# One more seven-product unit in the up-projection of an encoder trunk

## The chip, the cores and the metric

The kernel runs on one core of one Trainium2 chip. The metric is the device time of one launch in microseconds (us); lower is better. An execution under the hardware profiler gives the trace that all readings come from.

## The reference, cut to what matters

A trunk of two layers over 256 positions of width 2048, all in float32. Layer 0 mixes tokens with grouped-query attention, layer 1 with dilated window attention; each is followed by a gated MLP. Only the MLP's first step is touched by the change:

```python
def conv_ffn(h, w_up, conv_w, conv_b, w_down):
    u = h @ w_up                       # [256, 2048] @ [2048, 2 * 5632]
    u = depthwise_conv3(u, conv_w) + conv_b
    gate, val = split(u, 2)
    return (silu(gate) * val) @ w_down

for i in range(2):                     # layers
    h = h + mixer_i(rms_norm(h))
    h = h + conv_ffn(rms_norm(h), ...)
```

## The kernel before

**Three matmuls for one product.** Every float32 operand is split into two parts, a high one (`wh`, `xh`) and the rest (`wl`, `xl`). A product is then three matmuls on TensorE (PE), written in lines 135 to 137: `xh*wh`, `xh*wl`, `xl*wh`. The activations are the operand that is loaded into the array, the weights stream through it, 512 columns at a time. A weight tile of 128x1024 is loaded from memory by a DMA that SP issues into a tile `raw`; ScalarE (ACT) rounds it to `wh` (line 147), VectorE (DVE) subtracts to get `wl` (line 148). There are four `wh` and four `wl` tiles in rotation (`NHL`), so splits can run at most four tiles ahead of PE, and four `raw` tiles plus two extra ones.

**Tiling of the up-projection.** The 22 column blocks of 512 are taken as 11 pairs p, gate block p and value block 11+p. The first half has p = 0 to 5, the second 6 to 10; after each half the down-projection of that half runs. The inner dimension of 2048 is cut into four chunks kg of 512. In a plain pair (`project` twice, with `feed` for each chunk) the gate block runs through its four chunks and is handed to `gate_done`, then the value block does. One chunk of one block is 24 matmuls with 2 split weight tiles; of both blocks, 48 matmuls and 4 split tiles.

**The seven-product unit.** For the pairs in `UP` the function `up_pair` treats chunk 0 of gate and value together as a 2x2 block product in the Strassen-Winograd manner (`fast_unit`): seven products instead of eight. The activations' sums for it are made once per half, during p = 0 (lines 495 to 523, in the dictionary `picks`). The weights' four sums are made on DVE for every unit, in the `raw` tiles themselves (line 181), and each of the seven weight operands is split by ACT and DVE (lines 182 and 183). A unit is 42 matmuls (lines 189 to 191), 7 splits on each engine and 4 sums on DVE. Four of its products (numbers 1, 5, 6, 7) go to accumulators `ps` of their own; ACT copies number 1 out (line 547) and DVE folds them into the pair's four accumulators with eight additions (lines 549 to 557), so that the gate can be evacuated after the first four of these. The chunks run in `UP_ORDER`: gate chunks 1, 2, 3, the unit, value chunks 1, 2, 3.

**What else runs beside it.** `gate_gen` and `value_gen` are generators that are advanced a step at a time between the groups of matmuls: ACT evacuates an accumulator with the row's scale (line 492), DVE transposes 32x32 blocks (line 380), GpSimd (POOL) and ACT place them in `u` (line 632), ACT and DVE do the convolution (lines 612 and 620), ACT the silu (line 650), DVE the product with the gate (line 656) and the split of the result (ACT line 697, DVE line 698, or line 708 on where the chunk is one for a unit of the down-projection).

**What sets the order.** Each engine runs its own queue in order. The queue's order is made when the program is built, by a scheduler that follows the order in which the code emits; weight splits are emitted with a higher priority (`AHEAD`), so they stand earlier than the code says. `UP` also steers the generators: in `gate_gen` a gate in `UP` waits 3 steps (4 in one case) instead of 1 before the convolution of the value before it, and in `gate_done` such a gate goes into the list `beside`, which is advanced at other moments than `pending`.

Of the kernel before, what the change touches and what calls it, by code (L numbers as in the profile page):

```python
# [22 lines left out]
SCALE = 128.0 ** -0.5  # L23
NRAW, NHL = 4, 4
AHEAD = 60
UP = 2, 4, 6, 8
MIX = (0, 1), (0, 2), (1, 1), (1, 2)
MIX_ORDER = (1, 0), (2, 0), (3, 0), (1, 1), (2, 1), (0, None), (3, 1)
EVEN = range(0, 16, 2)
# [7 lines left out]
def tile_encoder(ctx: ExitStack, tc: tile.TileContext, x, xT, w_a, w_ao, q_gain, k_gain, w_b, w_bo,  # L37
# [265 lines left out]
    def project2(w, n0, n1, lhs, kgs, late, first_done, hook=None, cuts=(), drained=()):  # L303
        a0, a1 = new_acc(), new_acc()
        cuts = (0, *cuts, len(kgs) - late, len(kgs))
        for c0, c1 in zip(cuts, cuts[1:]):
            part, end = range(c0, c1), c1 == len(kgs)
            if end:
                drain()
                for gen in drained:  # L310
                    start(gen())
            for accs, n in ((a0, n0), (a1, n1)):
                for i in part:
                    kg = kgs[i]
                    mid = hook and hook(n == n0, kg)
                    feed(accs, lhs, kg, w[n, kg], i == 0, i == len(kgs) - 1,
                         pieces=4 if hook and i < 2 else 2 if hook else 1, mid=mid)
                if end and n == n0:
                    first_done(a0)
        return a1  # L320
# [204 lines left out]
    def up_pair(w, ns, lhs, order, picks, junk, fold_tile, first_done):  # L525
        (a2, a4), (a3, a8) = new_acc(), new_acc()
        acc, begun = {2: a2, 3: a3, 4: a4, 8: a8}, set()
        sides = (a2, a4), (a3, a8)
        tt = nc.vector.tensor_tensor
        for i, (kg, side) in enumerate(order):  # L530
            later = {s for _, s in order[i + 1:]}
            if side is None:
                acc.update({q: ps_tile() for q in (1, 5, 6, 7)})
                end = [q for q, s in ((1, None), (5, None), (6, None), (7, None), (2, 0), (4, 0), (3, 1))
                       if not later & {None, s}]
                fast_unit(acc, picks[kg], w[ns[0], kg], w[ns[1], kg], begun, end, None)
            else:
                mine = ((2, 4), (3, 8))[side]
                feed(sides[side], lhs, kg, w[ns[side], kg], not begun.issuperset(mine),
                     not later & {side, None}, begun=[m for m in range(2) if mine[m] in begun])  # L540
                begun.update(mine)
            if 0 in begun or not begun >= {1, 2} or later & {0, None}:
                continue
            begun.add(0)
            a, t = junk(), fold_tile()
            v, w_ = t[:, 0], t[:, 1]
            nc.scalar.activation(a, acc[1], AF.Copy)
            with tc.issue_after(newest[0].ins):
                tt(v, acc[6], a, ALU.subtract)
                tt(w_, acc[7], v, ALU.add)  # L550
                tt(a2, a2, a, ALU.add)
                tt(a4, a4, w_, ALU.subtract)
            first_done((a2, a4))
            tt(v, acc[5], v, ALU.add)
            tt(w_, acc[5], w_, ALU.add)
        tt(a3, a3, v, ALU.add)
        tt(a8, a8, w_, ALU.add)
        return a3, a8

    def ffn(l, hT, ss_in, cw, g_next, last, side=None):  # L560
        with tc.tile_pool(name=nm("fpool"), bufs=1) as fp:
# [63 lines left out]
            def turned(s, u, at_once=False):  # L625
                quad = quad_tile(fp, "quad", 2)
                for m in range(2):
                    quad_T(quad, slice(m, 8, 2), s[:, m])

                def move(i, put):  # L630
                    q, c = QC[i]
                    put(u[32 * c:32 * c + 32, :, :, 32 * q:32 * q + 32],  # L632
                        quad[32 * q:32 * q + 32, c].rearrange("p (j m) t -> p j m t", m=2))

                for i in range(0, 16, 2):
                    move(i, nc.gpsimd.tensor_copy)
                if not at_once:
                    yield
                for i in range(1, 16, 2):
                    move(i, partial(nc.scalar.activation, func=AF.Copy))  # L640

            def gate_gen(accs, blk, value):
                s = evac_scaled(fp, accs, rstd, 1)
                yield
                yield from turned(s, blk[1])
                if value is not None:
                    for _ in range(1 if blk[0] not in UP else 4 if value[5] // 4 - 1 in fast else 3):
                        yield
                    with tc.issue_after(evac[0].ins):
                        nc.scalar.activation(value[3], value[3], AF.Silu)  # L650
                    yield from product(value)
# [6 lines left out]
            def value_gen(accs, blk, gate, last):  # L658
# [10 lines left out]
                yield from turned(s, blk[1])  # L669
                wait = 5 if last is None or gate[0] + 1 in UP else 4 if gate[0] in UP else 2  # L670
                if gate[0] + 1 in UP and last is not None and last[5] // 4 in fast:
                    for _ in range(wait):
# [70 lines left out]
            for hf, (p0, p1) in enumerate(HALVES):  # L743
# [5 lines left out]
                for p in range(p0, p1):  # L749
# [5 lines left out]
                    def gate_done(accs, gate=gate, last_value=last_value):  # L755
                        gen = gate_gen(accs, gate, last_value)
                        if gate[0] in UP:
                            next(gen)
# [7 lines left out]
                    if p == 0:  # L766
                        va = project2(w_up[l], 0, NPAIR, hT, kgs, 1, gate_done, None, (), [first])
                    elif p in UP:
                        va = up_pair(w_up[l], (p, NPAIR + p), hT, UP_ORDER, picks, junk, st_tile, gate_done)
# [823 lines left out]
```

## Time and profile before

| | |
|---|---|
| median of 3 runs | 2221.86 us |
| the runs | 2221.15, 2221.86, 2224.96 us |
| span of the profiled execution, first to last instruction | 2220.5 us |
| PE busy | 2207.1 us (99%), 9933 matmuls |
| DVE busy | 1823.1 us (82%), 2295 instructions |
| ACT busy | 1528.2 us (69%), 2328 instructions |
| POOL busy | 546.1 us (25%) |
| DMA | 439.60 MB, mean 198 GB/s |

The profiled execution's own time is known only by its span; it is 0.65 us below the fastest of the three runs, which leaves room for no more than that around it. A row of groups reads: line, engine, operation, output<-inputs, shapes, count | busy time, mean ns of one | idle time just before them and what ended it. A timeline row gives the start in us from the span's start, the length in us, and the instruction, with xN for N of a kind in a row; idle time before it and its releaser stand in square brackets. Lengths of instructions on one engine overlap a little at their ends, so the distance of starts is shorter than the length; on PE it is much shorter. In the trace of layer 0, pair p = 1 begins at about 300 us and p = 2 at about 344 us; in layer 1 at about 1551 and 1594 us.

### The profile page before, as it was taken

What the parts mean: (1) busy time and instruction counts of PE and PEld (TensorE: products, weight loads), DVE (VectorE), ACT (ScalarE), POOL (GpSimd) and SP (SyncE); (2) the same over time, 40 slices, a digit from 0 to 9 for tenths busy, and PEclk for the clock granted to TensorE, in tenths of its full rate; (3) what the DMA queues carried; (4) which work ended last, traced back from release to release, by engine and by line L of the source; (5) the groups of instructions that cost most, each with busy time, mean ns of one, the idle gap of its engine ahead of it and who ended that gap; (6) DMA issues with size and microseconds to landing.
All of it is one profiled execution on the core that took longest, in us unless ns stands there. A gap on an engine that the chain in (4) does not pass through costs nothing.

```text
span 2220.5 us, 28992 instructions
## 1 busy us (share of the span) xinstructions
PE 2207.1 (99%) x9933; PEld 1828.5 (82%) x9933; DVE 1823.1 (82%) x2295; ACT 1528.2 (69%) x2328; POOL 546.1 (25%) x793
## 2 busy tenths in 40 slices
PE   9999999999999999999999999999999999999998
PEld 7888888888888888888888888888888888888887
DVE  6877669899897998868876878587798998879887
ACT  7666677787457787677756775567777855678764
POOL 3343222321003221042354216003222300212211
PEclk9999999999999999999999999999999999999999
DMA  8665665656656566665666555556555565656754
GB/s 305 192 220 184 216 188 190 201 189 196 203 181 222 186 205 200 204 202 195 183 199 199 174 180 189 190 184 214 181 202 194 192 209 190 217 162 218 224 193 143
DMA packets 126181, 439.60 MB, mean 198 GB/s; under 512 B 14408, under 2 KB 18248, under 8 KB 126032
## 3 DMA queue, kind: packets, MB, share of 16 engines
q1 hardware_dynamic: 123056, 429.05, 59.2%
q0 software_dynamic: 2688, 8.39, 1.5%
q8 instruction: 78, 1.28, 0.2%
q14 instruction: 71, 0.58, 0.1%
q10 hardware_dynamic: 288, 0.30, 0.0%
HBM read 432.34 MB, written 5.34 MB: 197 GB/s over the span
## 4 chain that ended last, share of the span: by engine, by line
PE 54%; POOL 1%; issue 1%; DMA 0%; ACT 0%; DVE 0%; POOLq 0%; DVEq 0%; ACTq 0%
PE acc L136 15%; PE acc L135 15%; PE acc L137 15%; PE ps L190 1%; PE ps L189 1%; PE ps L191 1%; PE acc L190 1%; PE acc L189 1%; PE acc L191 1%; DMA raw<-in_w_b_dram 0%; POOL wide L399 0%; PE ps L1422 0%; PE ps L342 0%; POOL wide L384 0%; ACT wh L147 0%
## 5 line engine op out<-in xcount | busy, mean ns | idle before, releaser
L148 DVE TENSOR_TENSOR wl<-raw,wh 128x1024 fp32r<-128x1024 f32 (+1 forms) x700 | 858.9, 1237 | 257.6 <-ACT wh L147 253.1
L147 ACT ACTIVATE wh<-raw 128x1024 fp32r<-128x1024 f32 (+1 forms) x700 | 726.8, 1046 | 342.5 <-PE acc L137 240.6
L136 PE MATMUL acc<-wl,xh 128*128 128x512 f32 x1984 | 773.8, 390 | 1.5 <-DVE wl L148 1.4
L135 PE MATMUL acc<-wh,xh 128*128 128x512 f32 x1984 | 773.7, 390 | 0.5 <-ACT wh L147 0.5
L137 PE MATMUL acc<-wh,xh 128*128 128x512 f32 x1984 | 772.1, 389 | 0.0
L136 PEld LDWEIGHTS acc<-wl,xh 128*128 128x128 f32 x1984 | 372.6, 188 | 81.5 <-DVE wl L148 5.7
L135 PEld LDWEIGHTS acc<-wh,xh 128*128 128x128 f32 x1984 | 372.5, 188 | 77.4 <-ACT wh L147 1.0
L137 PEld LDWEIGHTS acc<-wh,xh 128*128 128x128 f32 x1984 | 372.4, 188 | 76.9
L632 POOL COPY u<-quad 32x256 f32<-32x256 f32 x352 | 237.7, 675 | 702.5 <-DVE quad L380 684.4
L135 PE MATMUL acc<-wh,a 128*128 128x512 f32 x720 | 280.9, 390 | 0.0
L136 PE MATMUL acc<-wl,a 128*128 128x512 f32 x720 | 280.3, 389 | 0.0
L137 PE MATMUL acc<-wh,a 128*128 128x512 f32 x720 | 280.0, 389 | 0.0
L182 ACT ACTIVATE wh<-raw 128x1024 fp32r<-128x1024 f32 x140 | 148.5, 1061 | 122.4 <-PE acc L137 102.6
L183 DVE TENSOR_TENSOR wl<-raw,wh 128x1024 fp32r<-128x1024 f32 x140 | 166.9, 1218 | 6.3 <-ACT wh L182 5.8
L632 ACT ACTIVATE u<-quad 32x256 f32<-32x256 f32 x352 | 147.8, 420 | 23.2 <-DVE quad L380 18.7
L137 PEld LDWEIGHTS acc<-wh,a 128*128 128x128 f32 x720 | 135.1, 188 | 28.3 <-DVE a L331 0.2
L135 PEld LDWEIGHTS acc<-wh,a 128*128 128x128 f32 x720 | 135.2, 188 | 27.7
L136 PEld LDWEIGHTS acc<-wl,a 128*128 128x128 f32 x720 | 135.2, 188 | 27.6 <-DVE wl L148 0.3
L399 POOL COPY wide<-quad 32x256 f32<-32x256 f32 x88 | 54.8, 622 | 234.8 <-DVE quad L380 167.8
L492 ACT ACTIVATE stg<-acc,rstd 128x512 f32<-128x512 f32 x122 | 81.9, 685 | 32.9 <-PE acc L137 21.3
L384 POOL COPY wide<-quad 32x256 f32<-32x256 f32 x133 | 89.8, 675 | 41.4 <-DVE quad L380 32.0
L380 DVE STREAM_TRANSPOSE quad<-stg 128x512 f32<-128x512 f32 x112 | 75.7, 696 | 11.6 <-ACT stg L492 11.4
(318 smaller groups left out, 2444.5 us busy)
## 6 DMA issues: line engine op xcount, KB each, us to landing
raw<-in_w_up_dram SPq DMA_DIRECT2D x352, 512.0 KB, 4.6
raw<-in_w_down_dram SPq DMA_DIRECT2D x176, 512.0 KB, 4.6
raw<-in_w_b_dram SPq DMA_DIRECT2D x144, 512.0 KB, 4.6
raw<-in_w_bo_dram SPq DMA_DIRECT2D x48, 512.0 KB, 4.4
raw<-in_w_a_dram SPq DMA_DIRECT2D x40, 512.0 KB, 4.7
raw<-in_w_ao_dram SPq DMA_DIRECT2D x32, 512.0 KB, 4.5
raw<-in_w_a_dram SPq DMA_DIRECT2D x16, 256.0 KB, 5.8
there<-quad POOLq DMA_DIRECT2D x6, 512.0 KB, 3.7
```

Source lines behind the costliest of these rows:

```text
L135: nc.tensor.matmul(accs[m], xh, wh[:, j, :], start=st, stop=False)
L136: nc.tensor.matmul(accs[m], xh, wl[:, j, :], start=False, stop=False)
L137: nc.tensor.matmul(accs[m], xl, wh[:, j, :], start=False, stop=sp)
L147: nc.scalar.activation(wh[:, c], r[:, c], AF.Copy)
L148: newest[0] = nc.vector.tensor_tensor(wl[:, c], r[:, c], wh[:, c].bitcast(F32), ALU.subtract)
L182: nc.scalar.activation(wh, r, AF.Copy)
L183: newest[0] = nc.vector.tensor_tensor(wl, r, wh.bitcast(F32), ALU.subtract)
L380: nc.vector.transpose(quad[:, :, at, :], src.rearrange("p (x c t) -> p c x t", c=4, t=32))
L384: nc.gpsimd.tensor_copy(o[32 * c:32 * c + 32, :, 32 * q:32 * q + 32], quad[32 * q:32 * q + 32, c])
L399: nc.gpsimd.tensor_copy(dst, src)
L492: evac[0] = nc.scalar.activation(o[:, m, :], accs[m], AF.Copy, scale=rstd[:, m:m + 1])
L632: put(u[32 * c:32 * c + 32, :, :, 32 * q:32 * q + 32], quad[32 * q:32 * q + 32, c].rearrange("p (j m) t -> p j m t", m=2))
```

## The change

The tuple of pairs that go through `up_pair` gets a fifth member, 1:

```diff
-UP = 2, 4, 6, 8
+UP = 1, 2, 4, 6, 8
```

With it p = 1 of each layer goes through `up_pair` instead of two calls of `project`: one more unit per layer, two in the program. Pairs 1 and 2 are now both unit pairs, where before a plain pair lay between any two of them in the first half. In all, PE's queue has 12 rows fewer (9790 to 9778), DVE's 30 instructions more, ACT's 8 more. POOL's queue is the same; SP issues as many loads, eight of them from line 170 instead of line 125.

On DVE, in layer 0, this is what stands before where p = 1 reaches its last gate chunk (`cg`, `u`: the convolution of p = 0's gate):

```order
L148 TENSOR_TENSOR wl_3109<-raw_3092,wh_3108 128x1024
L148 TENSOR_TENSOR wl_3129<-raw_3124,wh_3128 128x1024
L620 SCALAR_TENSOR_TENSOR cg_2641<-u_2636,cw_555,cg_2641 128x256 x4
L148 TENSOR_TENSOR wl_3147<-raw_3126,wh_3146 128x1024
L620 SCALAR_TENSOR_TENSOR cg_2641<-u_2636,cw_555,cg_2641 128x256 x4
L148 TENSOR_TENSOR wl_3178<-raw_3173,wh_3177 128x1024
L148 TENSOR_TENSOR wl_3209<-raw_3175,wh_3208 128x1024
```

And at the same place in the changed program, where the unit of p = 1 now stands (`raw<-raw,raw` are the weights' sums):

```order
L148 TENSOR_TENSOR wl_3111<-raw_3092,wh_3110 128x1024
L183 TENSOR_TENSOR wl_3139<-raw_3130,wh_3138 128x1024
L181 TENSOR_TENSOR raw_3130<-raw_3130,raw_3136 128x1024
L181 TENSOR_TENSOR raw_3136<-raw_3136,raw_3134 128x1024
L183 TENSOR_TENSOR wl_3149<-raw_3132,wh_3148 128x1024
L183 TENSOR_TENSOR wl_3159<-raw_3134,wh_3158 128x1024
L181 TENSOR_TENSOR raw_3134<-raw_3130,raw_3134 128x1024
L181 TENSOR_TENSOR raw_3132<-raw_3134,raw_3132 128x1024
L183 TENSOR_TENSOR wl_3170<-raw_3130,wh_3169 128x1024
L183 TENSOR_TENSOR wl_3181<-raw_3136,wh_3180 128x1024
L183 TENSOR_TENSOR wl_3192<-raw_3134,wh_3191 128x1024
L183 TENSOR_TENSOR wl_3203<-raw_3132,wh_3202 128x1024
```

Eleven operations of 128x1024 take the place of four splits, and the gate's convolution has moved behind the unit.

On DVE, in the unit of p = 2 that follows, the order before was this (`wl_3515` is its first weight operand, `wl_3579` its last):

```order
L183 TENSOR_TENSOR wl_3515<-raw_3506,wh_3514 128x1024
L181 TENSOR_TENSOR raw_3506<-raw_3506,raw_3512 128x1024
L181 TENSOR_TENSOR raw_3512<-raw_3512,raw_3510 128x1024
L183 TENSOR_TENSOR wl_3525<-raw_3508,wh_3524 128x1024
L183 TENSOR_TENSOR wl_3535<-raw_3510,wh_3534 128x1024
L181 TENSOR_TENSOR raw_3510<-raw_3506,raw_3510 128x1024
L181 TENSOR_TENSOR raw_3508<-raw_3510,raw_3508 128x1024
L183 TENSOR_TENSOR wl_3546<-raw_3506,wh_3545 128x1024
L183 TENSOR_TENSOR wl_3557<-raw_3512,wh_3556 128x1024
L183 TENSOR_TENSOR wl_3568<-raw_3510,wh_3567 128x1024
L183 TENSOR_TENSOR wl_3579<-raw_3508,wh_3578 128x1024
```

In the changed program the same unit (now `wl_3540` to `wl_3604`) stands like this:

```order
L183 TENSOR_TENSOR wl_3540<-raw_3531,wh_3539 128x1024
L183 TENSOR_TENSOR wl_3550<-raw_3533,wh_3549 128x1024
L181 TENSOR_TENSOR raw_3531<-raw_3531,raw_3537 128x1024
L183 TENSOR_TENSOR wl_3560<-raw_3535,wh_3559 128x1024
L181 TENSOR_TENSOR raw_3537<-raw_3537,raw_3535 128x1024
L183 TENSOR_TENSOR wl_3571<-raw_3531,wh_3570 128x1024
L181 TENSOR_TENSOR raw_3535<-raw_3531,raw_3535 128x1024
L183 TENSOR_TENSOR wl_3582<-raw_3537,wh_3581 128x1024
L181 TENSOR_TENSOR raw_3533<-raw_3535,raw_3533 128x1024
L183 TENSOR_TENSOR wl_3593<-raw_3535,wh_3592 128x1024
L620 SCALAR_TENSOR_TENSOR cg_2993<-u_2635,cw_555,cg_2993 128x256
L183 TENSOR_TENSOR wl_3604<-raw_3533,wh_3603 128x1024
```

The eleven operations are the same, but each sum now stands directly ahead of the split that needs it, and a piece of a convolution has come in between.

On PE, at the end of that unit, the order before was (products number 6 in `ps`, then number 4 in `acc`, then the plain chunk of line 135):

```order
L189 MATMUL ps_3504<-wh_3567,s_2951 128x512
L190 MATMUL ps_3504<-wl_3568,s_2951 128x512
L191 MATMUL ps_3504<-wh_3567,s_2952 128x512
L189 MATMUL acc_3360<-wh_3578,xh_2293 128x512
L190 MATMUL acc_3360<-wl_3579,xh_2293 128x512
```

In the changed program two matmuls that need only a `wh` stand ahead of ones that need a `wl`:

```order
L189 MATMUL ps_3529<-wh_3592,s_2951 128x512
L189 MATMUL acc_3380<-wh_3603,xh_2293 128x512
L190 MATMUL ps_3529<-wl_3593,s_2951 128x512
L191 MATMUL ps_3529<-wh_3592,s_2952 128x512
L189 MATMUL ps_3529<-wh_3592,s_2951 128x512
L190 MATMUL ps_3529<-wl_3593,s_2951 128x512
L191 MATMUL ps_3529<-wh_3592,s_2952 128x512
L135 MATMUL acc_3381<-wh_3629,xh_2391 128x512
L190 MATMUL acc_3380<-wl_3604,xh_2293 128x512
```

The last product's first matmul with `wl_3604` has moved one place behind a matmul of the next chunk.

## Prediction

> **What bounds the kernel now.** I read the page's busy times first, then PE's row of the waits, then PE's timeline, and then DVE's windows, groups and timeline around p = 1 and p = 2.
>
> ```profile
> PE 2207.1 (99%) x9933; PEld 1828.5 (82%) x9933; DVE 1823.1 (82%) x2295; ACT 1528.2 (69%) x2328; POOL 546.1 (25%) x793
> ```
>
> PE is the bound: 99% of a span of 2220.5 us. The waits of PE over the whole program confirm it:
>
> ```profile
> PE ps L346 <- DVE qTl L331: 2.2, 2, 2.0
> PE ps L452 <- DVE warm L449: 1.5, 1, 1.5
> PE acc L136 <- DVE wl L148: 1.4, 4, 0.5
> PE acc L135 <- ACT wh L147: 0.5, 1, 0.5
> ```
>
> All visible waits of PE add to about 6 us. So a matmul that goes shortens the time, and a wait that comes lengthens it by its full size. The price of a matmul is not the 390 ns that its groups show, since matmuls overlap. It is the distance of starts:
>
> ```profile
> 329.68 0.39 PE L136 MATMUL acc<-wl,xh 128*128 128x512 f32 x1
> ...
> 342.37 0.39 PE L135 MATMUL acc<-wh,xh 128*128 128x512 f32 x1
> ```
>
> The second row is the 56th matmul after the first: 12.69 / 56 = 0.2267 us each.
>
> **What the change removes.** A chunk of a gate and value pair is 48 matmuls, a unit 42. Two units take away 12 matmuls, 12 x 0.2267 = 2.72 us, 0.12% of the time. That is the most that it can bring: 1.36 us in each layer. About 0.2% (4.4 us) is what a measurement of this kernel tells from no change, so a clear gain would need something beyond the removed matmuls, and I see nothing.
>
> **What it adds, on DVE.** The stretch that matters runs from where DVE would make the first split of the new unit (310.4 us in layer 0, 1560.7 in layer 1) to its last split for the unit of p = 2:
>
> ```profile
> core 0: us, DVE busy (x), PEclk, DMA share, GB/s
> 310.40:367.60 57.20, 45.51 (x57) 1.00 0.53 167
> 1560.70:1618.00 57.30, 45.47 (x57) 1.00 0.54 167
> ```
>
> DVE works 45.5 of 57.2 us there and idles 11.7. The groups of the same stretch tell the prices and the idle time:
>
> ```profile
> L148 DVE TENSOR_TENSOR wl<-raw,wh 128x1024 fp32r<-128x1024 f32 x16 | 19.8, 1243 | 10.7 <-ACT wh L147 10.7
> L183 DVE TENSOR_TENSOR wl<-raw,wh 128x1024 fp32r<-128x1024 f32 x7 | 8.2, 1218 | 0.0
> L181 DVE TENSOR_TENSOR raw<-raw,raw 128x1024 f32<-128x1024 f32 x4 | 4.9, 1225 | 0.1
> L698 DVE TENSOR_TENSOR a<-cv,a 128x256 fp32r<-128x256 f32 x4 | 1.7, 454 | 0.9 <-ACT a L697 0.9
> ```
>
> Step by step, for one layer:
> - Splits: seven for four, 3 x 8.2 / 7 = 3.5 us.
> - Sums of weights: 4 x 4.9 / 4 = 4.9 us.
> - Eight fold additions. In the unit of p = 2 they stand like this on DVE's timeline:
>
> ```profile
> 363.03 4.62 DVE L183 TENSOR_TENSOR wl<-raw,wh 128x1024 fp32r<-128x1024 f32 x4
> 367.57 0.69 DVE L551 TENSOR_TENSOR acc<-acc,junk 128x512 f32<-128x512 f32 x1
> ...
> 373.40 0.67 DVE L552 TENSOR_TENSOR acc<-acc,fold 128x512 f32<-128x512 f32 x1
> 373.97 0.67 DVE L554 TENSOR_TENSOR fold<-ps,fold 128x512 f32<-128x512 f32 x1
> 374.57 0.67 DVE L555 TENSOR_TENSOR fold<-ps,fold 128x512 f32<-128x512 f32 x1
> 376.81 0.71 DVE L380 STREAM_TRANSPOSE quad<-stg 128x512 f32<-128x512 f32 x1 [1.56 <-ACT stg L492]
> ```
>
>   Back to back they start 0.57 to 0.60 us apart, alone they take 0.69: 8 x 0.64 = 5.1 us.
>
> Together 13.5 us. The rest of DVE's work is the same set between the two places: convolution pieces stand later in the new order, but ahead of the same last split. So DVE needs 45.5 + 13.5 = 59.0 us, and has 57.2 - 1.36 = 55.8. It falls short by 3.2 us. It also had a lead to lose at the end:
>
> ```profile
> 368.50 0.39 PE L190 MATMUL acc<-wl,xh 128*128 128x512 f32 x1
> ```
>
> This is PE's first use of the unit's last `wl`; DVE had it at 363.03 + 4.62 = 367.65, so the lead was 0.85 us. PE's new order moves this use back by one matmul, 0.23 more. Unhidden remain 3.2 - 0.85 - 0.23 = 2.1 us per layer, if DVE does not idle for a moment. That is the lower end. DVE cannot save up for it: the splits run at most four tiles ahead, and the 10.7 us that it waited for ACT's `wh` were mostly waits for PE to free such a tile.
>
> The upper end adds the idle time that may survive. After the unit of p = 2, DVE waited 1.56 us for ACT to evacuate the gate (the row at 376.81), because ACT stood before a split whose weights had not landed:
>
> ```profile
> ACT wh L147 <- DMA raw<-in_w_up_dram: 3.8, 1, 3.8
> DVE quad L380 <- ACT stg L492: 1.6, 1, 1.6
> PEld acc L136 <- DVE wl L148: 0.9, 1, 0.9
> ```
>
> The unit holds four `raw` tiles to its end, so no load can start, and then they start late. On DVE and ACT the operations behind the new unit stand in the same order as behind that one, so I expect this wait of about 1.5 us again, now in a stretch that has no idle time to give. Another 0.9 is the wait for ACT's line 697. So DVE makes PE wait 2.1 to 2.1 + 1.5 + 0.9 = 4.5 us per layer. I take 3.7, the lower end with the first of the two waits: its place is the same, while convolution pieces now fill the second.
>
> **What hides.** The copies on ACT have these rows:
>
> ```profile
> L182 ACT ACTIVATE wh<-raw 128x1024 fp32r<-128x1024 f32 x140 | 148.5, 1061 | 122.4 <-PE acc L137 102.6 <-PE ps L191 8.4 <-issue 4.8
> L547 ACT ACTIVATE junk<-ps 128x512 f32<-128x512 f32 x12 | 7.0, 580 | 0.0
> ```
>
> A unit adds three copies and one evacuation, 3 x 1.06 + 0.58 = 3.8 us; ACT is busy 42.8 of the 57.2 us and has room:
>
> ```profile
> 310.40:367.60 57.20, 57.20 (x254) 47.22 (x253) 45.51 (x57) 42.82 (x63) 9.94 (x16) 1.00 0.53 167
> ```
>
> (The columns are the stretch, PE, weight loads, DVE, ACT, POOL.) If that cover were gone, its splits would be late by what is missing, and DVE's with them. SP issues as many loads, in another order; POOL's queue does not change. The sums of the activations are made for p = 2 already. The gate of p = 1 is ready 114 matmuls into the pair instead of 96; its accumulator is wanted by nobody before p = 2. The new unit itself should not make PE wait: it is entered with the lead that the unit of p = 2 had, and that one cost nothing.
>
> **The sum.** -2.72 + 2 x 3.7 = +4.7 us. The profiled execution spans 2220.5 us, 0.65 below the fastest run and 1.4 below the median of 2221.86; the sum against the span is 2225.2, and against the median that is compared, 2226.5 us. That is 0.2% slower, at the edge of what shows. With the two ends of the wait the time is 2221.86 - 2.72 + 2 x 2.1 = 2223.3, and 2221.86 - 2.72 + 2 x 4.5 = 2228.1.
>
> **The rivals.**
>
> *The cover holds.* DVE's 11.7 us of idle time are more than three quarters of the 13.5 us that are added, and part of the folds could slip behind the last split. If the lead carries the rest, the full 2.72 us stay: 2219.1. It decides whether DVE's added work ahead of the last split of p = 2 stays under 11.7 - 1.36 + 0.85 = 11.2 us. Against it: by the new order all of the 13.5 stand ahead.
>
> *Only the gap of the loads counts.* DVE keeps up, but each new unit costs the wait for the weights behind it. That was 0.9 us in layer 0 (the row of PEld above). Twice: -2.72 + 1.8, 2220.9. For it speaks that this wait is the only one of PE that the trace has near a unit here.
>
> *DVE slows while POOL copies.* Two spells of POOL's eight copies lie in the stretch of each layer. DVE and POOL at such places:
>
> ```profile
> 345.55 5.35 POOL L632 COPY u<-quad 32x256 f32<-32x256 f32 x8 [16.46 <-DVE quad L380]
> 377.65 7.40 POOL L632 COPY u<-quad 32x256 f32<-32x256 f32 x8 [26.75 <-DVE quad L380]
> ```
>
> ```profile
> 345.61 1.42 DVE L148 TENSOR_TENSOR wl<-raw,wh 128x1024 fp32r<-128x1024 f32 x1 [0.19 <-ACT wh L147]
> 368.17 2.35 DVE L148 TENSOR_TENSOR wl<-raw,wh 128x1024 fp32r<-128x1024 f32 x2
> ...
> 377.44 3.86 DVE L148 TENSOR_TENSOR wl<-raw,wh 128x1024 fp32r<-128x1024 f32 x3
> 381.23 2.22 DVE L620 SCALAR_TENSOR_TENSOR cg<-u,cw,cg 128x256 f32<-128x256 f32 x4
> ```
>
> ```profile
> 353.00 1.67 DVE L620 SCALAR_TENSOR_TENSOR cg<-u,cw,cg 128x256 f32<-128x256 f32 x4
> ```
>
> Where DVE had no gaps, behind 377, three splits took 3.86 us, against 1.5 x 2.35 = 3.53 without POOL, and four convolution pieces 2.22 against 1.67; POOL's copies stretched from 5.35 to 7.40. That is 0.9 us lost in one spell. With two such spells in a stretch that is now full, each layer loses up to 1.8 us more: 2226.5 + 3.6 = 2230.1. The page "SBUF — State Buffer" of the Trainium skill (section "SBUF: two separate sides") says that DVE operations with two inputs from SBUF and GpSimd operations share a port pair as an exclusive lock, and whichever starts second blocks for the whole instruction of the other. By that rule the sixteen copies of a stretch could hold DVE for all of POOL's 9.94 us, and the sum would be up to 2226.5 + 2 x 9.94 = 2246.4. The rows agree that there is a loss, though with 1.42 against 1.18 us for a split it is far less than a whole copy.
>
> **How the numbers follow.** The forecast (DVE short, 2223.3 to 2228.1 about 2226.5): 0.59. The cover holds, 2219.1: 0.12. Only the loads' gap, 2220.9: 0.11. POOL's slowing on top, 2230.1: 0.18. Slower by over 0.2% means over 2226.3: all of the last, and about half of the first, 0.47. Faster by over 0.2% is out of reach of 12 matmuls; 0.03 for runs that scatter. Within: 0.50. The range leaves out most of the case in which the cover holds, and ends just above the last: 2220.3 to 2231.0.
>
> **What would show it.** Right: PE with 9921 matmuls in rows 0.2267 us apart, a new wait of PE for DVE's `wl` of line 183 inside the unit of p = 2 (about 358 to 372 us, and 1250 us later in layer 1), 2 to 4 us in each layer, DVE busy without gaps from the new unit to there, and no new wait in the unit of p = 1. Wrong: PE without new waits (then DVE had more room than its rows say), a wait for DMA instead, or a wait in p = 3 or later, where I count none.

## The result, and the profile after

The changed kernel takes 2227.37 us (median of 21 runs, 2224.63 to 2229.3). The kernel before, run beside it, takes 2223.87 us (21 runs, 2221.15 to 2226.72; the three runs shown above are among these, two of them at its lower end). The ratio is 1.0014, 95% interval [1.0007, 1.0020]: slower by 3.1 us by the ratio and by 3.5 by the medians. I had predicted 2226.5 us. The interval leaves out 1, so 0.14% does show here; I had named 0.2% as the edge.

The profiled execution of the changed kernel spans 2225.1 us, and its time was 2226.85. In all its 21 runs the time is 1.7 to 1.8 us above the span. So the profile of before, with its span of 2220.5, was an execution of about 2222.3 us (an estimate from these), near the median of its three runs and not below the fastest. The busy times after:

```profile
PE 2207.5 (99%) x9921; PEld 1826.2 (82%) x9921; DVE 1850.2 (83%) x2325; ACT 1533.8 (69%) x2336; POOL 549.8 (25%) x793
```

PE has the 12 matmuls less. The span is longer all the same, and PE's waits over the whole program say for whom:

```profile
PE ps L346 <- DVE qTl L331: 2.5, 2, 2.0
PE ps L190 <- DVE wl L183: 2.4, 4, 0.6
PE acc L136 <- DVE wl L148: 1.8, 5, 0.6
...
PE acc L189 <- ACT wh L182: 1.3, 2, 0.7
```

Lines 189 and 190 are a unit; they were not in this list before. PE's timeline shows the place in layer 0, the unit of p = 2:

```profile
363.30 0.39 PE L189 MATMUL acc<-wh,s 128*128 128x512 f32 x1
363.96 0.50 PE L190 MATMUL acc<-wl,s 128*128 128x512 f32 x1 [0.27 <-DVE wl L183]
...
365.22 0.40 PE L189 MATMUL ps<-wh,s 128*128 128x512 f32 x1
366.23 0.50 PE L190 MATMUL ps<-wl,s 128*128 128x512 f32 x1 [0.61 <-DVE wl L183]
...
367.49 0.40 PE L189 MATMUL ps<-wh,s 128*128 128x512 f32 x1
368.50 0.50 PE L190 MATMUL ps<-wl,s 128*128 128x512 f32 x1 [0.61 <-DVE wl L183]
...
369.76 0.40 PE L189 MATMUL ps<-wh,s 128*128 128x512 f32 x1
370.81 0.50 PE L189 MATMUL acc<-wh,xh 128*128 128x512 f32 x1 [0.65 <-ACT wh L182]
```

The brackets understate the loss, since the matmul before counts as busy to its modelled end. The starts tell it: they stand 0.66, 1.01, 1.01 and 1.05 us apart where 0.227 is normal, and behind each of the four late matmuls the next start is about 0.335 us away, 0.11 more than normal. The excess is 3.25 us. In layer 1 the same sum is 2.80 us. So -2.72 + 3.25 + 2.80 = +3.3 us, and the runs say +3.1 to +3.5.

DVE, from the first split of the new unit to the last split of p = 2's unit (columns: the stretch, PE, weight loads, DVE, ACT, POOL, each with its count, then PEclk, DMA share, GB/s), has no room left:

```profile
312.29:372.25 59.96, 57.82 (x251) 46.61 (x250) 59.29 (x72) 45.51 (x65) 11.74 (x16) 1.00 0.50 168
1564.07:1623.58 59.51, 57.64 (x251) 46.61 (x250) 59.18 (x72) 45.47 (x65) 11.45 (x16) 1.00 0.50 170
```

It is busy for 59.29 of 59.96 us, where it was busy for 45.51 of 57.20 before. Its timeline behind the first unit, and at the end of that stretch:

```profile
333.30 0.71 DVE L380 STREAM_TRANSPOSE quad<-stg 128x512 f32<-128x512 f32 x1 [0.33 <-ACT stg L492]
333.94 3.85 DVE L148 TENSOR_TENSOR wl<-raw,wh 128x1024 fp32r<-128x1024 f32 x3
337.72 3.30 DVE L620 SCALAR_TENSOR_TENSOR cg<-u,cw,cg 128x256 f32<-128x256 f32 x6
...
359.29 2.35 DVE L183 TENSOR_TENSOR wl<-raw,wh 128x1024 fp32r<-128x1024 f32 x2
361.56 1.21 DVE L181 TENSOR_TENSOR raw<-raw,raw 128x1024 f32<-128x1024 f32 x1
362.69 1.21 DVE L183 TENSOR_TENSOR wl<-raw,wh 128x1024 fp32r<-128x1024 f32 x1
...
370.64 0.48 DVE L620 SCALAR_TENSOR_TENSOR cg<-u,cw,cg 128x256 f32<-128x256 f32 x1
371.03 1.22 DVE L183 TENSOR_TENSOR wl<-raw,wh 128x1024 fp32r<-128x1024 f32 x1
```

Between 361 and 370 us a sum and a split alternate at 1.13 us each: 2.27 us of DVE for a product that PE does in six matmuls, 1.36 us. That is the rhythm of PE's waits, which come 2.27 us apart.

### The profile page after: what moved, and what is told of

Same layout as the page of the kernel before. It is cut to its first block, busy times and chain, and to the rows that moved or that the text cites. A ratio compares the mean times of both kernels' runs of the same rounds, so it can differ in the third digit from the quotient of the medians.

```text
span 2225.1 us, 29023 instructions
## 1 busy us (share of the span) xinstructions
PE 2207.5 (99%) x9921; PEld 1826.2 (82%) x9921; DVE 1850.2 (83%) x2325; ACT 1533.8 (69%) x2336; POOL 549.8 (25%) x793
## 4 chain that ended last, share of the span: by engine, by line
PE 94%; DVE 2%; DMA 1%; POOL 1%; issue 1%; ACT 1%; SPq 0%; DVEq 0%; POOLq 0%; ACTq 0%
PE acc L136 27%; PE acc L137 27%; PE acc L135 27%; PE ps L190 2%; PE ps L191 2%; PE ps L189 2%; PE acc L189 2%; PE acc L190 2%; PE acc L191 2%; DVE wl L148 1%; DMA raw<-in_w_a_dram 1%; DVE raw L181 0%; PE ps L346 0%; DVE wl L183 0%; PE ps L345 0%
## 5 line engine op out<-in xcount | busy, mean ns | idle before, releaser
L147 ACT ACTIVATE wh<-raw 128x1024 fp32r<-128x1024 f32 (+1 forms) x692 | 718.1, 1046 | 336.1 <-PE acc L137 233.2
L136 PE MATMUL acc<-wl,xh 128*128 128x512 f32 x1952 | 761.2, 390 | 1.2 <-DVE wl L148 1.2
L135 PE MATMUL acc<-wh,xh 128*128 128x512 f32 x1952 | 761.3, 390 | 0.2 <-ACT wh L147 0.2
L137 PE MATMUL acc<-wh,xh 128*128 128x512 f32 x1952 | 759.7, 389 | 0.0
L136 PEld LDWEIGHTS acc<-wl,xh 128*128 128x128 f32 x1952 | 366.8, 188 | 79.8 <-DVE wl L148 5.4
L135 PEld LDWEIGHTS acc<-wh,xh 128*128 128x128 f32 x1952 | 366.7, 188 | 75.8 <-ACT wh L147 0.7
L137 PEld LDWEIGHTS acc<-wh,xh 128*128 128x128 f32 x1952 | 366.5, 188 | 75.8
L632 POOL COPY u<-quad 32x256 f32<-32x256 f32 x352 | 242.2, 688 | 702.6 <-DVE quad L380 684.6
L182 ACT ACTIVATE wh<-raw 128x1024 fp32r<-128x1024 f32 x154 | 162.8, 1060 | 133.8 <-PE acc L137 97.4
L183 DVE TENSOR_TENSOR wl<-raw,wh 128x1024 fp32r<-128x1024 f32 x154 | 184.0, 1220 | 7.0 <-ACT wh L182 6.5
L181 DVE TENSOR_TENSOR raw<-raw,raw 128x1024 f32<-128x1024 f32 x70 | 86.7, 1239 | 1.4
```

The costliest lines, as they stand in the source:

```text
L135: nc.tensor.matmul(accs[m], xh, wh[:, j, :], start=st, stop=False)
L136: nc.tensor.matmul(accs[m], xh, wl[:, j, :], start=False, stop=False)
L137: nc.tensor.matmul(accs[m], xl, wh[:, j, :], start=False, stop=sp)
L147: nc.scalar.activation(wh[:, c], r[:, c], AF.Copy)
L182: nc.scalar.activation(wh, r, AF.Copy)
L183: newest[0] = nc.vector.tensor_tensor(wl, r, wh.bitcast(F32), ALU.subtract)
```

## The experiments

Two measures go through all of them. **PE's loss** in a place is the sum over its matmuls of the distance to the next start, less 0.2267 us, where that distance is over 0.25. **DVE's stretch** is the time from the first split of p = 1's unit to the end of the last split of p = 2's unit, from the same view as the two rows above. Each kernel was timed beside the kernel before, and the ratios are to that. The edits are shown against the changed kernel, cut to the lines or parts of lines that differ.

### The unit of p = 1 without that of p = 2

```diff
-UP = 1, 2, 4, 6, 8
+UP = 1, 4, 6, 8
```

> The unit of p = 2 becomes a plain pair, the new unit of p = 1 stays (pairs 1, 4, 6, 8): as many units and matmuls (9933) as before. Theory DVE is short between two neighbouring units: no neighbour, so no wait of PE above 0.5 us between 300 and 400 us or between 1550 and 1650 us; time as before the change (about 2223.9 by 21 runs), within 1 us. Rival, the unit of p = 1 costs something by itself (its later gate, the generators' other steps): some 1.5 us per layer, 3 us slower than before, with waits of PE in p = 1 or p = 3.

2221.85 us, ratio 0.9996 [0.9987, 1.0005]. PE's waits over the whole program hold no line of a unit:

```profile
PE acc L136 <- DVE wl L148: 2.1, 5, 0.8
PE ps L346 <- DVE qTl L331: 2.0, 1, 2.0
PE ps L452 <- DVE warm L449: 1.5, 1, 1.5
PE acc L135 <- ACT wh L147: 0.5, 1, 0.5
```

So the new unit in its place costs PE nothing by itself; the loss needs the second unit behind it.

### A plain pair between all the units

```diff
-UP = 1, 2, 4, 6, 8
+UP = 1, 3, 5, 6, 8
```

> Three units in the first half as after the change, but with a plain pair between any two (pairs 1, 3, 5, 6, 8): 9921 matmuls. Theory DVE is short between neighbours: the waits of 3 us per layer go, under 0.7 us remain at each unit; 2.0 to 2.7 us faster than before, about 2221.5, and 5 us faster than the changed kernel. Rival, a third unit in a half is too much for DVE wherever it stands: about 3 us of waits of PE per layer again, 2227.

2230.75 us, ratio 1.0034 [1.0023, 1.0046]: slower, and a miss. PE loses nothing in the units of p = 1 and p = 3, but 1.5 us at 436 to 446 us, in the chunks behind the unit of p = 3, and 3.5 us between 530 and 558 us; in layer 1 the two are 1.6 and 3.3. Most of the second loss lies in a unit of the down-projection, which begins at 546 us. PE's groups there:

```profile
L190 PE MATMUL ps<-wl,s 128*128 128x512 f32 x6 | 2.7, 446 | 1.8 <-DVE wl L183 1.8
```

The unit of p = 5 ends at 502 us, 45 us ahead of that one; between the units of p = 1 and p = 2 lie 33. I had looked for neighbours in the up-projection only. A plain pair between units is thus no safeguard. What DVE lacked in these places was not taken apart.

### Less work for DVE: a tap of the convolution left out

For the columns of p = 0 alone, one outer tap of the convolution is left out: eight operations of DVE less in each layer.

```diff
-for i, o in ((0, 0), (2, 1)):
+for i, o in ((0, 0), (2, 1))[:1 if n in (0, NPAIR) else 2]:
```

> The changed kernel with one of the convolution's outer taps left out for p = 0 alone, gate and value: eight DVE operations of 128x256 fewer between the two units, 8 x 0.43 = 3.5 us per layer, everything else as in the changed kernel, and each sum still directly ahead of its split. Theory DVE's total is short by 3 us per layer: the waits in the unit of p = 2 (3.25 and 2.80 us in the changed kernel) shrink to under 0.7, time about 2221.5. Rival, the order of sums and splits inside the unit of p = 2 makes the waits: they stay at 2.5 to 3.3, time about 2227.

2223.99 us, ratio 1.0002 [0.9993, 1.0011]. PE's loss fell from 3.25 and 2.80 to 2.1 us in each layer, neither to nothing nor by nothing: theory and rival both missed the size. Where the rest of the 3.5 us went, DVE's stretch and its timeline tell:

```profile
310.38:369.21 58.83, 57.55 (x251) 46.69 (x250) 55.74 (x64) 45.59 (x65) 11.51 (x16) 1.00 0.49 171
```

```profile
337.37 1.02 DVE L620 SCALAR_TENSOR_TENSOR cg<-u,cw,cg 128x256 f32<-128x256 f32 x2 [0.52 <-ACT cg L612]
338.81 2.36 DVE L148 TENSOR_TENSOR wl<-raw,wh 128x1024 fp32r<-128x1024 f32 x2 [0.42 <-ACT wh L147]
342.63 0.48 DVE L620 SCALAR_TENSOR_TENSOR cv<-u,cw,cv 128x256 f32<-128x256 f32 x1 [1.45 <-ACT cv L612]
```

DVE has 3.5 us less to do and idles 3.1 instead of 0.7 us: relieved, it waits for ACT, mostly for ACT's part of the convolution. The stretch is only 1.13 us shorter, and PE's loss 1.15. So work taken away counts only where DVE can do the next thing at once; my expectation had counted every microsecond of it.

### The order of sums and splits put back

The sums in the units are held to their old, earlier places.

```diff
-                if q in sums:
+                if q in sums and spot is not None:
...
+                if spot is None:
+                    tc.keep_in_program_order(newest[0])
+                for early in ((3, 5), (), (7, 6))[i] if spot is None and i < 3 else ():
+                    tc.keep_in_program_order(nc.vector.tensor_tensor(*sums[early], ALU.add))
```

> The changed kernel with the order of the four sums in the unit of p = 2 put back to that of before (split 1, two sums, splits 2 and 3, two sums, four splits); the same instructions. Theory DVE's total is short: PE waits as long in sum, 2.5 to 3.3 us per layer, only at other products (the second and the fourth); time about 2227. Rival, the order makes the waits: they go, about 2221.5.

2245.89 us, ratio 1.0101 [1.0085, 1.0116]. In the unit of p = 2 the waits stand at other products, and PE loses 3.3 us in layer 0: the alternation is how the shortage shows, not its cause. Most of the 22 us were lost elsewhere, which I had not foreseen: the same function makes the units of layer 1's mixer, and there the forced order made PE wait about 2 us twice in each of three units (1028, 1079 and 1292 us). In layer 1 the unit of p = 2 lost 3.6 us.

### Part of DVE's work given to GpSimd

```diff
-nc.vector.tensor_tensor(cv, cg, cv, ALU.mult)
+(nc.gpsimd if n == NPAIR else nc.vector).tensor_tensor(cv, cg, cv, ALU.mult)
...
-nc.vector.tensor_tensor(lo, cv[:, j, :], hi.bitcast(F32), ALU.subtract)
+eng = nc.gpsimd if value[0] == NPAIR else nc.vector
+eng.tensor_tensor(lo, cv[:, j, :], hi.bitcast(F32), ALU.subtract)
```

> The changed kernel, with the product of the value with the gate (line 656) and the four subtractions of line 698 for p = 0's result on GpSimd instead of DVE: 2.9 us of DVE's work less in each layer, between the two units. The output is the same. If DVE's work between the units decides (the theory), but DVE then waits elsewhere for its own inputs, as with the tap left out (3.5 us less work made the wait in the unit about 1 us shorter), the wait of PE in the unit of p = 2 falls from about 3 to about 2 us in each layer: 2225.4 against 2227.4 of the changed kernel. If DVE is slowed by GpSimd's work beside it (the rival), the wait stays or grows, and the time is 2227.4 or more.

2229.08 us, ratio 1.0031 [1.0018, 1.0043]; PE's loss grew to 4.9 and 4.8 us. The outcome is the rival's. Of the 2.9 us that were taken off DVE, its busy time in the stretch fell by 0.75 only (59.29 to 58.54), and its idle time rose by 2.4. POOL's timeline (line 699 is the subtraction), then DVE's:

```profile
346.40 3.22 POOL L656 TENSOR_TENSOR cv<-cg,cv 128x1024 f32<-128x1024 f32 x1 [7.28 <-DVE cv L620]
...
357.41 2.48 POOL L699 TENSOR_TENSOR a<-cv,a 128x256 fp32r<-128x256 f32 x2
```

```profile
347.88 2.83 DVE L148 TENSOR_TENSOR wl<-raw,wh 128x1024 fp32r<-128x1024 f32 x1
...
357.12 1.28 DVE L183 TENSOR_TENSOR wl<-raw,wh 128x1024 fp32r<-128x1024 f32 x1 [2.69 <-ACT wh L182]
358.33 0.96 DVE L620 SCALAR_TENSOR_TENSOR cg<-u,cw,cg 128x256 f32<-128x256 f32 x1
359.21 1.76 DVE L183 TENSOR_TENSOR wl<-raw,wh 128x1024 fp32r<-128x1024 f32 x1
```

The split that began beside POOL's product took 2.83 instead of 1.22 us, and ended 1.09 us after it (346.40 + 3.22 = 349.62; 347.88 + 2.83 = 350.71). The one at 359.21 ended 1.08 us after POOL's subtractions. About 1.1 us is the distance at which splits follow each other: as if these two had begun only when POOL was done. The page "SBUF — State Buffer" of the Trainium skill (section "SBUF: two separate sides") says this of a DVE operation with two inputs from SBUF against one of GpSimd; the trace agrees. Ahead of the unit DVE, relieved, waited 2.69 us for the first `wh`, which ACT made 45.3 us into the stretch, as late as in the changed kernel (45.2).

POOL is only part of the cause, since the edit changed DVE's order too. Three pieces of the convolution of p = 1's gate that stood ahead of the unit's first split now stand inside the unit, 0.4 us each. From that split on DVE lost 1.1 us beside POOL's subtractions and 1.2 on these pieces, and it had begun 0.6 earlier: together the 1.6 to 1.7 us by which PE's loss and the stretch grew. What POOL alone would have cost or saved, no run shows.

### The unit of p = 2 one chunk later

```diff
+LATE_ORDER = (1, 0), (2, 0), (3, 0), (1, 1), (0, None), (2, 1), (3, 1)
...
-... UP_ORDER, picks, junk, st_tile, gate_done)
+... LATE_ORDER if p == 2 else UP_ORDER, picks, junk, st_tile, gate_done)
```

> The changed kernel, with the unit of p = 2 one value chunk later in its pair: 24 matmuls, 5.4 us, in which DVE has two more splits (2.4 us) to make. The same instructions otherwise. If DVE's shortage at a deadline is the cause (the theory), 3.0 us more room covers the 2.8 to 3.25 us that were missing, PE's wait in that unit falls below 0.7 us in each layer, and the time is about 2223.9 - 2.7 + 0.7 = 2222, up to 2 us below the kernel before. If the unit is short within itself whenever sums and splits alternate (2.27 us of DVE for a product against 1.36 of PE: the rival), the wait stays at 2 us or more in each layer, and the time at 2225 or more.

2224.03 us, ratio 1.0004 [0.9995, 1.0013]. (Here, and in the next but one, the last operations of p = 1's value convolution and the product with the gate come after the split of the result has begun; number and kinds of operations are the same.) PE's loss in the unit fell to 1.9 us in each layer, and the gap of 0.7 us behind it went. That is between the theory (under 0.7) and the rival (2 or more). The place does matter; but in DVE's stretch stood six operations more, not the two that I had counted: besides two splits four more pieces of the convolution of p = 1's gate, which had moved ahead into the room.

### The unit of p = 1 earlier

```diff
+EARLY_ORDER = (1, 0), (0, None), (2, 0), (3, 0), (1, 1), (2, 1), (3, 1)
...
-... UP_ORDER, picks, junk, st_tile, gate_done)
+... EARLY_ORDER if p == 1 else UP_ORDER, picks, junk, st_tile, gate_done)
```

> The changed kernel, with the new unit of p = 1 two gate chunks earlier in its pair: 48 matmuls (10.9 us) more between the units, in which DVE has four splits (4.7 us) to make, so 6 us more room ahead of the unit of p = 2. The same instructions otherwise. By the theory of the deadline the wait in the unit of p = 2 goes, and the time is 2221 to 2222, unless the earlier unit of p = 1 now comes too soon after p = 0 and makes a wait of its own. By the rival (short within the unit) the wait stays at 2 us or more in each layer, 2225 or more.

2229.89 us, ratio 1.0035 [1.0023, 1.0048]. A miss for the theory as it stood. PE loses 3.3 and 3.5 us in p = 2, no less than in the changed kernel, and 1.6 more in p = 1 in each layer, whose unit now stands close behind p = 0. DVE's stretch, and one row of its timeline:

```profile
299.10:371.80 72.70, 69.41 (x299) 55.44 (x299) 65.59 (x78) 55.88 (x83) 22.91 (x28) 1.00 0.49 166
```

```profile
337.02 1.23 DVE L148 TENSOR_TENSOR wl<-raw,wh 128x1024 fp32r<-128x1024 f32 x1 [3.06 <-ACT wh L147]
```

DVE idles 7.1 us in it, most of that ahead of 338 us; from there to the last split it is busy for 32.0 of 33.6 us, nearly as full as in the changed kernel. Room that is given 35 us ahead of the deadline is idled away: DVE cannot split more than four tiles ahead, and cannot do a convolution whose inputs are not there. So what counts here is the work of the last 30 us or so; the length is read off this one run.

### Later unit and GpSimd together

> Both at once: the unit of p = 2 one chunk later, and 2.9 us of DVE's work on GpSimd. By the theory the wait is gone already with the later unit, so this adds nothing: 2221 to 2222. If the later unit alone leaves a wait, this one shows whether DVE's work takes the rest away. If GpSimd's work slows DVE, it is slower than the later unit alone.

2227.85 us, ratio 1.0024 [1.0016, 1.0033]; PE loses 3.6 us in the unit in each layer against 1.9 with the later unit alone. Work on GpSimd made it worse in this place as in the other, and here too three pieces of the convolution moved behind a split that they stood ahead of, so POOL's share is again about 1 us and not the whole.

### The convolution behind the unit

This takes the later unit and two edits in the generators: the convolution of p = 1's gate comes three steps later, the product with it two steps earlier.

```diff
-wait = 5 if last is None ...
+wait = 8 if gate[0] == 1 else 5 if last is None ...
...
-... range(1 if blk[0] not in UP else 4 ...
+... range(1 if blk[0] not in UP or blk[0] == 2 else 4 ...
```

> The changed kernel with the unit of p = 2 one value chunk later, the convolution of p = 1's gate behind that unit instead of ahead of it (three steps more of its generator), and two steps less of waiting in p = 2's gate generator, so that p = 1's result is ready in time. All the work is there. The later unit by itself brought the wait of PE in p = 2 from 3.3 and 2.8 to 1.9 us in each layer, not to nothing, and in its order six more operations stood ahead of the last split than in the changed kernel: two splits and four pieces of that convolution. If DVE's work in the last 25 us ahead of the last split decides (the theory), 3.0 us of room and 1.6 us of pieces that are gone cover the whole wait: under 0.3 us in each layer, and about 2223.9 - 2.7 - 0.4 = 2220.8, faster than both. If only a third of what is freed can be used, as the two runs that freed work seemed to say (the rival), 1.5 us stay in each layer and the time is 2223.5 or more.

2223.76 us, ratio 1.0003 [0.9994, 1.0012]. (In this one the silu is taken of a gate whose last four pieces of convolution come after it; the operations are all there.) The unit is cured, with 0.4 and 0.1 us lost. But the time is that of the rival, since a new wait stands 20 us behind the unit, where the plain chunks now need their `wl`; DVE, then PE:

```profile
389.02 1.66 DVE L620 SCALAR_TENSOR_TENSOR cg<-u,cw,cg 128x256 f32<-128x256 f32 x4
390.61 3.24 DVE L620 SCALAR_TENSOR_TENSOR cv<-u,cw,cv 128x256 f32<-128x256 f32 x8
393.78 1.21 DVE L148 TENSOR_TENSOR wl<-raw,wh 128x1024 fp32r<-128x1024 f32 x1
```

```profile
393.71 0.39 PE L135 MATMUL acc<-wh,xh 128*128 128x512 f32 x1
395.04 0.50 PE L136 MATMUL acc<-wl,xh 128*128 128x512 f32 x1 [0.94 <-DVE wl L148]
```

Twelve pieces of convolution in a row, 4.8 us, hold up a split that was wanted at 393.9. PE loses 1.2 us there, and 1.7 in layer 1.

### Only the convolution later

```diff
-wait = 5 if last is None ...
+wait = 7 if gate[0] == 1 else 5 if last is None ...
```

> The changed kernel with both units where they are, and only the convolution of p = 1's gate two steps of its generator later, so that none of its four pieces of 0.4 us stands ahead of the last split of p = 2's unit. By the theory PE's wait in that unit falls by the 1.6 us of these pieces, from 3.3 and 2.8 to about 1.7 and 1.2 us, and the time by 3.2 us, to 2224.2. By the rival (a third can be used) it falls by 0.5 us in each layer, to 2226.3.

2225.76 us, ratio 1.0013 [1.0005, 1.0022]: nearer to the rival. PE loses 2.1 us in the unit in each layer, 1.15 and 0.7 less, where I had expected 1.6; the pieces that are gone were in part replaced by waits of DVE. Behind the unit it loses 1.1 and 1.3 us, against 0.75 and none in the changed kernel. The first half of the convolution must go somewhere, and the chunks right behind the unit are no better.

### Half of it, or all of it, behind a later unit, and the rest spread

Both have the unit of p = 2 one chunk later. The first keeps half of that convolution ahead of the unit; the second has all of it behind, and what follows on it later. All the work is done in its order in both.

```diff
-wait = 5 if last is None ...
+wait = 7 if gate[0] == 1 else 5 if last is None ...
...
+for _ in range(2 if gate[0] == 2 else 0):
+    yield
```

The second has 8 for the 7, and beside the same two lines this:

```diff
-... range(1 if blk[0] not in UP else 4 ...
+... range(2 if blk[0] == 2 else 1 if blk[0] not in UP else 4 ...
```

> The changed kernel with the unit of p = 2 one value chunk later; of the convolution of p = 1's gate four pieces stay ahead of that unit's last split and four come behind it, and the split of p = 1's result comes two steps later, so that the work behind the unit is spread further than with the whole convolution behind it. All the work is there. With the unit later and eight pieces ahead, PE waited 1.9 us in the unit in each layer; four pieces less are 1.6 us, so by the theory 0.3 us are left. With the whole convolution behind the unit, new waits of 0.8 to 1.6 us came some 22 us later; with half of it behind and the rest spread, I expect under 0.5 us there. Sum: 2223.9 - 2.7 + 2 x (0.3 + 0.3) = about 2222, 1 us below the kernel before. If PE's wait is only moved about by each move of DVE's work (the rival: the stretch as a whole is short), the waits add up to 1.5 us or more in each layer again, and the time is 2223.5 or more.

> As the other of this pair, but the whole convolution of p = 1's gate behind the unit and p = 1's value convolution one step later than in the run before with that convolution behind. All the work is there. By the theory the wait in the unit stays under 0.5 us in each layer; behind it the pieces are spread by two chunks more, so the new waits of 0.8 to 1.6 us shrink to under 0.5: about 2222. By the rival they stay, 2223.5 or more.

The first: 2222.08 us, ratio 0.9998 [0.9989, 1.0007]. PE loses 1.4 us in the unit in each layer and nothing behind it. The time is that of the theory, but not by its working: the loss of 1.4 is close to the rival's 1.5 and far from the 0.3 expected, and what the theory had too low there it had too high behind the unit. The second: 2221.66 us, ratio 0.9990 [0.9981, 0.9999], the lowest of all medians (by 0.2 us, which is no clear difference to the unit of p = 1 alone), and just faster than the kernel before. PE loses nothing in the unit, and 0.6 us in each layer some 17 to 25 us behind it. (Its profiled execution spans 2222.0 us, not less than that of before; 1.6 us of that are the slow matmuls of the last section.) PE's waits are the four lines of the unit of p = 1 alone (the last with 0.4 us for 0.5), none of them of a unit, and DVE's unit stands in the old order again:

```profile
360.79 1.21 DVE L183 TENSOR_TENSOR wl<-raw,wh 128x1024 fp32r<-128x1024 f32 x1
362.04 2.49 DVE L181 TENSOR_TENSOR raw<-raw,raw 128x1024 f32<-128x1024 f32 x2
364.44 2.35 DVE L183 TENSOR_TENSOR wl<-raw,wh 128x1024 fp32r<-128x1024 f32 x2
366.83 2.49 DVE L181 TENSOR_TENSOR raw<-raw,raw 128x1024 f32<-128x1024 f32 x2
369.23 4.62 DVE L183 TENSOR_TENSOR wl<-raw,wh 128x1024 fp32r<-128x1024 f32 x4
```

### All of them in one table

DVE's stretch and PE's loss in the unit of p = 2, layer 0, in us. The last column is the stretch less the loss.

| kernel | stretch | of it DVE idle | PE's loss | difference |
|---|---|---|---|---|
| changed | 59.96 | 0.7 | 3.25 | 56.7 |
| tap left out | 58.83 | 3.1 | 2.1 | 56.7 |
| convolution later | 58.61 | 0.8 | 2.1 | 56.5 |
| sums put back | 59.98 | 0.45 | 3.3 | 56.7 |
| work to GpSimd | 61.65 | 3.1 | 4.9 | 56.8 |
| unit later | 63.38 | 0.35 | 1.9 | 61.5 |
| and work to GpSimd | 65.14 | 2.8 | 3.6 | 61.6 |
| and convolution behind | 61.68 | 1.3 | 0.4 | 61.3 |
| and half of it behind | 62.62 | 1.0 | 1.35 | 61.3 |
| and all of it, rest spread | 61.31 | 1.1 | 0.0 | 61.3 |

Among kernels with the unit in the same place the difference is constant within 0.3 us: PE waits for just as long as DVE's stretch exceeds it. Whether DVE works or idles in the stretch makes no difference to that.

In part this is arithmetic: where PE waits up to the last split, its time to that point is its own work plus its loss, and must end with DVE's. The table does not prove by itself which engine holds up which. That is shown by what releases PE's waits (DVE's `wl`, and for one ACT's `wh`, which had waited for DVE's sum) and by the runs in which DVE's work alone was moved.

The runs also show what a microsecond of moved work is worth. Against the same kernel without the move, the stretch of layer 0 lost 1.5 us of DVE's work with only the convolution later, 1.4 with half of it behind the later unit, 2.8 with all of it behind and the rest spread. PE's loss fell by 1.1, 0.5 and 1.8 us, mostly because DVE idled more in each. That is a third to three quarters, neither the whole that the theory counted nor always the rival's third.

## Why the prediction was right, step by step

- **PE's saving** is as worked out: 9921 matmuls, 2.72 us.
- **DVE's need**: 59.0 us forecast, 59.29 and 59.18 measured. The rise is 13.8 us for the 13.5 of the prediction.
- **DVE's room**: 55.8 us and leads of 0.85 and 0.23, together 56.9, from the rows of the kernel before. The table has 56.7, from the rows of the others. This was the step on which most hung, and it held.
- **Surviving idle time** was the term that I mis-sized. I took 1.5 us for the wait on ACT's evacuation behind the new unit. It came to 0.33 in layer 0 (the row at 333.30) and to none in layer 1. DVE reached that place 7.6 us behind the unit's last split, as it had behind the unit of p = 2 before, with the same operations. It was ACT that came earlier. ACT, before and then after:

```profile
374.19 2.01 ACT L147 ACTIVATE wh<-raw 128x1024 fp32r<-128x1024 f32 x2 [3.77 <-DMA raw<-in_w_up_dram]
```

```profile
331.63 1.06 ACT L147 ACTIVATE wh<-raw 128x1024 fp32r<-128x1024 f32 x1 [2.11 <-DMA raw<-in_w_up_dram]
```

Before, the two roundings just ahead of the evacuation both came behind the late weights; now one of the two had its weights in time, and only the other came late. Why that load came in time was not taken apart. I had also taken layer 0's figure for both layers, though in layer 1 of the kernel before the same wait is 0.30 us. The wait for line 697 fell from 0.9 to 0.2. All idle time in layer 0's stretch is 0.67 us, and these two are 0.53 of it. So PE lost 3.25 and 2.80 us, between my lower end of 2.1 and the 3.7 that I took.
- **The sum**: +3.3 us by the two traces' places against +4.7 forecast; the runs say +3.1 to +3.5. That the forecast of 2226.5 lies within 0.9 us of the measured 2227.37 is luck in part: the kernel before took 2.0 us more in 21 runs than in the three that I started from, which makes up for a sum that was 1.4 too high. That the profiled span met 2225.2 so closely (2225.1) is luck too: 1.9 us of its difference to the span before arose ahead of p = 1, where the change does nothing.
- **What hides** did hide. The unit of p = 1 has no wait (the first experiment shows it alone), and the waits of ACT inside the second unit are for DVE's sums:

```profile
ACT wh L182 <- DVE raw L181: 5.6, 4, 2.4
```

- **The rivals.** That the cover holds is out: PE lost 6.05 us in the two units. The loads' gap stayed as it was: behind p = 2's unit PE lost 0.77 us before and 0.75 now, and none behind p = 1's. That GpSimd's copies slow DVE is real but small in sum: three splits took 3.85 us beside them (the row at 333.94) as they had before, six pieces of convolution 3.30 where 1.67 for four would give 2.5. DVE's whole need came out only 0.3 above a sum that left this out, far from the 9.94 us that sixteen whole copies would have cost; what else became cheaper was not taken apart.

What I did not foresee is why DVE's shortage is so hard to mend. I had treated the stretch as one account. The runs showed that its early part cannot be saved for its late part.

## What to carry to other kernels

Where one engine prepares operands for another with a fixed number of buffers, cost the time from the last point at which it was ahead to each deadline; in these runs a microsecond too long there was a microsecond of waiting, busy or idle. Taking work away, or making room far ahead, helps only as far as the engine then has something to do. Moving work that nobody waits for behind the deadline helped by a third to three quarters of its size, until it held up the next one. So the added fast unit brought a gain only once the work around it had been moved: the order alone turned a ratio to the kernel before of 1.0014 into 0.9990, with the same matmuls.

## What the hardware showed that I had not expected

**TensorE can fall to half clock after a wait of 2 us, and where the wait falls decides it.** In every profile PE waits 2.2 to 2.3 us, by the starts, at about 142 us. In five of the fourteen profiles the granted clock then stands at 0.50 for 3.41 us, and six to eight matmuls follow each other at 0.427 us instead of 0.227; in the other nine none does. The traces' clock records lie on a grid: between the first rise to full clock and each later fall there is a whole number of steps of 3.413 us (in the unit of p = 1 alone the rise is at 4.71 us and the fall at 144.66, 41 steps later). In the five profiles the whole wait lies in one step, and PE is busy for 1.44 to 1.47 us of that step. In the nine others the wait lies across two steps, and PE is busy for at least 1.72 us in each. The step with most of the wait in the kernel before, then the step with the wait and the one behind it in the unit of p = 1 alone (PEclk is the third number from the end):

```profile
141.92:145.34 3.42, 2.06 (x11) 1.82 (x12) 3.42 (x5) 0.01 (x1) 0.00 (x0) 1.00 0.21 83
```

```profile
141.25:144.66 3.41, 1.45 (x9) 1.13 (x9) 3.41 (x6) 1.51 (x3) 1.40 (x1) 1.00 0.56 167
144.66:148.07 3.41, 3.41 (x10) 2.70 (x9) 1.97 (x5) 1.31 (x5) 0.00 (x0) 0.50 0.68 181
```

The fall costs 1.3 to 1.6 us in a run, about as much as the effects studied here, and half a microsecond decides: a wait that began 1.0 us into its step brought the fall (half of the convolution behind), one that began 1.6 us into it did not (the tap left out). So a single profile's span says little, and places in it say more. With the sums' order put back it happened in layer 1 too, behind each of the three pairs of waits of about 2 us that stand 3 us apart. In that run a step with 1.67 us busy was followed by a fall and one with 1.64 was not; PE's modelled ends blur the border. The page "TensorE: Matmul & The Clock Gate" (section "Part 1: The HAM clock gate") of the Trainium skill puts the fall to half clock behind an idle window of about 3.4 us that runs freely. The traces agree with the two speeds and with a freely running window of that length, but the window need not be idle from end to end: here one that was busy for 1.45 us was enough.

**A tensor-tensor operation on GpSimd stops one on VectorE to its end, and the other way round.** In both layers of both runs with work on GpSimd, the two splits ended 1.08 to 1.09 us after GpSimd's operation. GpSimd's subtraction that began beside a split took 1.60 us instead of 0.74 and ended 0.6 after it. Not everything is stopped: beside GpSimd's product a fold into an accumulator (line 557) took its usual 0.69 us, and transposes, with one input, took 0.70 and 0.66 beside its subtractions.
